# Routed experts: how the first row tiles are filled, and when the residual is scaled

## The chip, the cores and the metric

The kernel runs on one core of a Trainium2 chip. It is one program for a whole network: a convolution block, a retention block, and two layers that each have an attention stage and a stage of 32 routed experts. The time is device microseconds (us) of one execution; lower is better. Three runs of the kernel before gave 2948.9, 2949.08 and 2956.04 us.

## The reference

Only the stage of the experts and the sum behind it matter here. Each token picks one of 4 groups and then 2 of the 8 experts of that group; an expert is a gated feed-forward (1024 to 512 to 1024), and its output is added to its tokens with a gate.

```python
def hier_moe(h, w_rg, b_rg, w_re, b_re, w1, w3, w2):
    ...                                    # router: expert (n, 2), gates (n, 2)
    order = jnp.argsort(flat_e)
    counts = jnp.bincount(flat_e, length=N_EXPERTS)
    ...                                    # tokens sorted by expert, empty slots left at token 0
    def run(args):
        xb, e = args
        return (jax.nn.silu(xb @ w1[e]) * (xb @ w3[e])) @ w2[e]
    ys = lax.map(run, (xs, block_e)).reshape(-1, d_)
    return jnp.zeros_like(h).at[slot_tok].add(ys * slot_gate[:, None])

# in each of the two layers l:
x = layer_norm(ALPHA * x + g1 * o_x, ln1_g[l], ln1_b[l])
hx = (x * (1 + sc2) + sh2).reshape(b_ * s_, d_)
...                                        # layer 0 also routes 256 context tokens
y = hier_moe(tokens, w_rg[l], b_rg[l], w_re[l], b_re[l], w1[l], w3[l], w2[l])
x = layer_norm(ALPHA * x + g2 * y[:b_ * s_].reshape(b_, s_, d_), ln2_g[l], ln2_b[l])
```

The kernel keeps `x` normalised but without `ln1_g` and `ln1_b`, so the last line needs `x * (ALPHA * ln1_g) + ALPHA * ln1_b`. The kernel calls this work on `x` the residual steps.

## The kernel before, in words

**Routing.** `route` works out where each token goes and ends with index lists on VectorE: `list0` holds for each of the 32 experts 128 row numbers (its first 128 tokens; an empty slot holds a number beyond the table, and the gather skips it), `list1` the places to scatter results to. The rows themselves lie in device memory, in `hxd`, 4 KB each.

**Experts.** `experts` goes through the 32 experts in a fixed order; `p` counts them. `fetch(p)` starts a gather of up to 128 rows into one of three row tiles `xg` (an indirect DMA that GpSimd issues). `prepare(p + 1, h)` turns half of the next expert's row tile on TensorE and copies it into `xT`: the first half on ScalarE, the second on VectorE (`self.turned` is that second copy). `narrow` computes 64 tokens: 64 small matmuls with w1 and w3 into two banks, Silu on ScalarE, a product `s` on VectorE, two transposes of `s`, a copy `sT` on VectorE, 16 matmuls with w2, a copy `y` on ScalarE, and a scatter. Where an expert has more than 64 tokens, a branch (`tc.If(v > BS)`) does the next 64 and so on; every engine passes this branch, and after it each waits until the others have done what stood ahead of it. While the first expert of a layer runs, `lists()` makes two more lists (`sw`, `gw`) for experts with over 128 tokens, in steps between its matmuls.

**Weights.** An expert has three tiles of 2 MB (w1, w3, w2), loaded in halves by `expert_tile` from the queue of SyncE (SP), at most four halves under way. There is room for eight tiles; a tile's load waits until TensorE is done with the tile eight places earlier. Eight are asked for before the first expert, three more behind each expert's branch.

**Residual.** `residual` is a generator that gets one step behind each expert. For each half `h` of the columns: two loads of 512 gains and offsets spread over 128 partitions (`res`, 256 KB each in the tile), then a scaling of both by ALPHA on VectorE (L1967), then one row tile of `x` per expert. Only the work on a row tile was tied to `self.turned` (a dependency that keeps it behind that copy). The other steps are put where the scheduler has place: it sorts each engine's instructions by its own estimate of when they are ready, within the stretch between two branches and with what has no open dependency pulled ahead.

**Start of a stage.** The row tiles lie in memory that the stage before used. `xg` is set to zero first (three memsets on GpSimd, L1891), since a gather leaves skipped rows as they are.

Of the kernel before, what the change touches and what calls it, by code (L numbers as in the profile page):

```python
# [14 lines left out]
I32 = mybir.dt.int32  # L15
# [6 lines left out]
P = 128  # L22
# [12 lines left out]

DEPTH = 3
PAGES = 23
ORDER = [g * EPG + i for i in range(EPG) for g in range(NG)]
BS = 64
NC_ = 2  # L40
# [78 lines left out]
class Net:  # L119
    GAIN, NP = 0.7, 13  # L120

    def __init__(self, ctx, tc, aps):
        self.ctx, self.tc, self.nc, self.a = ctx, tc, tc.nc, aps
        nc = self.nc
        self.n = 0
        self.cp = ctx.enter_context(tc.tile_pool(name="cp", bufs=1))
        self.ps = ctx.enter_context(tc.tile_pool(name="ps", bufs=8, space=PSUM))
        self.dp = ctx.enter_context(tc.tile_pool(name="dp", bufs=1, space=DRAM))
        self.ring = ctx.enter_context(tc.tile_pool(name="ring", bufs=4))
        lay, w = const_layout()  # L130
        self.clay = lay
        self.small = ctx.enter_context(tc.tile_pool(name="small", bufs=1))
        self.x = self.cp.tile([P, NT, D], F32, name="x")
        for t in range(NT):
            nc.sync.dma_start(self.x[:, t], aps["x"][0, t * P:(t + 1) * P])
        self.ident = self.const("ident", self.cp)
        self.ctx_t = self.cp.tile([P, NC_, D], F32, name="ctx_t")
        self.gate = self.cp.tile([P, NT + NC_, 2], F32, name="gate")
        self.place = self.cp.tile([P, 2 * (NT + NC_)], F32, name="place")
        self.lists = self.cp.tile([P, NE], I32, name="list0"), self.cp.tile([P, 2 * NE], I32, name="list1")  # L140
        self.cnt = self.cp.tile([P, NE], I32, name="cnt")
        self.bg = deque()
        self.credit, self.gain = 0.0, 0.65
        self.pre = {}
# [1519 lines left out]
    def route(self, l, nt):  # L1664
# [61 lines left out]
        nc.vector.scalar_tensor_tensor(f, u, half, f, op0=ALU.mult, op1=ALU.add)  # L1726
        ts(u, f, tok + 0.5, float(tok), op0=ALU.is_ge, op1=ALU.mult)
        tt(u, f, u, op=ALU.subtract)
        ts(f, f, 0.5, 1e6, op0=ALU.is_lt, op1=ALU.mult)
        nc.vector.scalar_tensor_tensor(self.lists[0], u, -1.0, f, op0=ALU.add, op1=ALU.add)  # L1730
        ts(m, v, 0.5, 1e6, op0=ALU.is_lt, op1=ALU.mult)
# [49 lines left out]
    def experts(self, l, nt):  # L1781
# [32 lines left out]
        def gather(x, src, idx):  # L1814
            nc.gpsimd.indirect_dma_start(out=x, out_offset=None, in_=src,  # L1815
                                         in_offset=bass.IndirectOffsetOnAxis(ap=idx, axis=0),
                                         bounds_check=src.shape[0] - 1, oob_is_err=False)

        def scatter(y, dst, idx):
            nc.gpsimd.indirect_dma_start(out=dst, out_offset=bass.IndirectOffsetOnAxis(ap=idx, axis=0), in_=y,  # L1820
                                         in_offset=None, bounds_check=dst.shape[0] - 1, oob_is_err=False)
# [11 lines left out]
        def narrow(xT, i, w1, w3, w2, aside=iter(()), turn=lambda h: None):  # L1833


            hs = [self.bank(), self.bank()]
            tok = slice(i * BS, (i + 1) * BS)
            for h, w in zip(hs, (w1, w3)):
                for k in range(KD):
                    for c in range(2):  # L1840
                        mm(h[c * BS:(c + 1) * BS, 0:256], lhsT=xT[:, k, tok], rhs=w[:, k, c * 256:(c + 1) * 256],  # L1841
                           start=k == 0, stop=k == KD - 1, skip_group_check=True, tile_position=(0, c * BS))
                    next(aside, None)
            deque(aside, 0)
            s = new("s", 256, 1)
            nc.scalar.activation(s, hs[0][:, :256], AF.Silu)  # L1846
            nc.vector.tensor_tensor(s, s, hs[1][:, :256], op=ALU.mult)  # L1847
            turn(0)
            sT = new("sT", 256, 1)
            vcopy(sT, flip(s, 2))  # L1850
            turn(1)
            b = self.bank()
            for k in range(4):
                o = (k % 2) * P + (k // 2) * BS
                for c in range(2):
                    mm(b[c * BS:(c + 1) * BS], lhsT=sT[:, o:o + BS], rhs=w2[:, 2 * k + c], start=k == 0, stop=k == 3,  # L1856
                       skip_group_check=True, tile_position=(0, c * BS))
            y = new("y", 512, 2)
            acopy(y, b)  # L1859
            return y  # L1860
# [24 lines left out]
            scatter(broad(xT, part), yw, idx)  # L1885

        col = lambda t, e, i, n: t[:, e * n + i:e * n + i + 1]
        AHEAD = 2
        xg = [bc.tile([P, D], F32, name=f"xg{i}") for i in range(AHEAD + 1)]
        for x in xg:  # L1890
            nc.gpsimd.memset(x, 0.0)  # L1891
        xT, vs = {}, {}

        def fetch(p):

            if p < NE:
                e = ORDER[p]
                vs[e] = nc.values_load(cnt[0:1, e:e + 1], min_val=0, max_val=tok)
                gather(xg[p % (AHEAD + 1)], hw, col(gidx, e, 0, 1))

        def prepare(p, h):

            if p < NE:
                x = xg[p % (AHEAD + 1)]
                c = slice(h * 512, (h + 1) * 512)
                if h == 0:
                    xT[p] = new("xT", D, 2)
                    acopy(xT[p][:, c], flip(x[:, c], 4))
                else:
                    self.turned = vcopy(xT[p][:, c], flip(x[:, c], 4)).ins  # L1910
# [13 lines left out]
        for p, e in enumerate(ORDER):  # L1924
            with tc.high_priority():
                fetch(p + AHEAD)
            w = [self.wt.pop((e, m)) for m in range(3)]
            part = lambda m, i, w=w: w[m][:, i]
            v, x = vs.pop(e), xT.pop(p).rearrange("p (k s) -> p k s", k=KD)
            label = f"more_{l}_{p}"  # L1930
            hint = lambda i: tc.mark_branch_hint_location(f"{label}_{i}", 0, engines=[mybir.EngineType.PE])
            if p:
                hint("")
            scatter(narrow(x, 0, *w, lists() if p == 0 else iter(()), lambda h: prepare(p + 1, h)), yd, col(sidx, e, 0, 2))

            with tc.If(v > BS, preferred_fallthrough_block=True, label=label + "_"):  # L1936
                hint(0)
                more = new("wx", D, 1)
                with tc.If(v > 2 * BS, preferred_fallthrough_block=False):
                    gather(more, hw, col(gw, e, 1, nt))  # L1940
                scatter(narrow(x, 1, *w), yd, col(sidx, e, 1, 2))
                with tc.If(v > 2 * BS, preferred_fallthrough_block=True, label=label + "_0"):
                    hint(1)
                    rows128(more, col(sw, e, 1, nt), part)
                    with tc.If(v > 4 * BS, preferred_fallthrough_block=True, label=label + "_1"):
                        hint(2)
                        gather(more, hw, col(gw, e, 2, nt))
                        rows128(more, col(sw, e, 2, nt), part)
                        with tc.If(v > 6 * BS, preferred_fallthrough_block=True, label=label + "_2"):
                            with tc.For_i(3, (v + 2 * BS - 1) // (2 * BS), 1) as i:  # L1950
                                block(more, e, i, part)
            while self.wq_ and self.wn < 3 * (p + 1) + 8:
                self.expert_tile()
            next(residual, None)
            if p == NE - 3:
                self.combine_start(l, nt)

    def residual(self, l, nt):

        nc = self.nc  # L1960
        vs = [self.tmp.tile([P, 512], F32, tag=f"res{i}", name=self.nm("res"), bufs=1) for i in range(2)]
        for h in range(2):
            for v, k in zip(vs, ("ln1_g_2", "ln1_b_2")):
                nc.sync.dma_start(v, self.a[k][l, h * 512:(h + 1) * 512].partition_broadcast(P))
            yield
            for v in vs:
                nc.vector.tensor_scalar(v, v, ALPHA, None, op0=ALU.mult)  # L1967
            for t in range(nt):
                yield
                xs = self.rows(t)[:, h * 512:(h + 1) * 512]  # L1970
                op = nc.vector.tensor_tensor(xs, xs, vs[0], op=ALU.mult)
                dep = mybir.DependencyInfo(mybir.DependencyClass.Sync, mybir.DependencyReason.DATA)
                self.tc.add_manual_dep(op.ins, self.turned.name, dep, reason="one tile with each expert")
                nc.vector.tensor_tensor(xs, xs, vs[1], op=ALU.add)

    def combine_start(self, l, nt):
# [82 lines left out]
```

## Time and profile before

| | us |
|---|---|
| median of three runs | 2949.08 |
| the profiled execution | 2948.09 |
| its span on the core | 2945.8 |
| experts of layer 0, first row tile's transposes | 1355.39 |
| experts of layer 1, first row tile's transposes | 2272.94 |
| TensorE matmuls busy | 2557.8 |
| VectorE busy | 1318.4 |
| GpSimd busy | 618.2 |

Times in the rows below are microseconds from the start of the span. PE is TensorE, DVE VectorE, ACT ScalarE, POOL GpSimd, SP SyncE; SPq is the queue that issues transfers. The 2.3 us between the span and the execution's own time lie outside what the engines do. Layer 0's experts stand at 1355 to 1925 us, layer 1's at 2273 to 2899 us.

### The profile page before, as it was taken

To read this page: it belongs to the slowest core of one execution; us is meant where nothing else is said; L and a number is where in the kernel's file an instruction comes from. 1 tells how busy PE (TensorE), PEld (TensorE's weight loads), DVE (VectorE), ACT (ScalarE), POOL (GpSimd) and SP (SyncE) were. 2 spreads that over 40 slices of the span, in tenths; PEclk is the share of its full clock that TensorE was granted. 3 is DMA by queue.
4 is the path that set the end of the run, shared out by engine and by line. 5 is a ranking of instruction groups with operands and counts; after the bars stand their busy time and mean duration, and the time that the engine had idled before them with its cause. 6 is when DMAs were issued, how large, how long until landed. Compare 5 with 4: busy or idle time off the path is not lost. (4 is left out here: it accounts for less than half of the span.)

```text
span 2945.8 us, 38452 instructions
## 1 busy us (share of the span) xinstructions
PE 2557.8 (87%) x14392; PEld 1673.1 (57%) x14392; DVE 1318.4 (45%) x2803; ACT 790.8 (27%) x1750; POOL 618.2 (21%) x577
## 2 busy tenths in 40 slices
PE   5899989999999899995988888878796798888884
PEld 4666657787776785673544444447565454344442
DVE  6999975455355636763111111164876111010104
ACT  5666643223223324420101101023341011010100
POOL 4777740000001200142111111010414111010101
PEclk9999999999999999997999999989897999999997
DMA  6121244424422127324999999842224899475995
GB/s 193 58 86 62 82 172 150 144 90 147 162 100 72 36 47 257 79 108 185 393 399 394 391 404 397 323 159 65 65 57 165 326 390 403 170 312 234 394 405 214
DMA packets 202089, 610.39 MB, mean 207 GB/s; under 512 B 38542, under 2 KB 64538, under 8 KB 168932
## 3 DMA queue, kind: packets, MB, share of 16 engines
q1 hardware_dynamic: 179780, 572.10, 51.4%
q0 software_dynamic: 20400, 31.48, 3.3%
q8 instruction: 194, 3.18, 0.4%
q10 hardware_dynamic: 1520, 2.03, 0.2%
q14 instruction: 195, 1.60, 0.1%
HBM read 611.85 MB, written 29.20 MB: 218 GB/s over the span
## 5 line engine op out<-in xcount | busy, mean ns | idle before, releaser
L1841 PE MATMUL ps<-w,xT 128*64 128x256 f32 x4928 | 570.6, 384 | 82.4 <-ACTq L1936 41.0
L1841 PEld LDWEIGHTS ps<-w,xT 128*64 128x64 f32 x4928 | 348.6, 137 | 313.4 <-ACTq L1936 84.2
L1847 DVE TENSOR_TENSOR s<-s,ps 128x256 f32<-128x256 f32 x77 | 32.5, 422 | 860.3 <-PE ps L1841 860.3
L1856 PE MATMUL ps<-w,sT 128*64 128x512 f32 x1232 | 284.1, 603 | 23.9 <-DVE sT L1850 13.7
L425 POOL TENSOR_TENSOR c<-c,q 128x512 f32<-128x512 f32 x190 | 254.9, 1342 | 107.0 <-ACT q L424 94.7
L431 DVE SCALAR_TENSOR_TENSOR ps<-u,dwT,ps 128x512 f32<-128x512 f32 x274 | 201.0, 744 | 0.7
L282 PE MATMUL ps<-w,w 128*128 128x512 f32 (+1 forms) x480 | 182.1, 381 | 14.1 <-ACT w L243 12.8
L297 DVE TENSOR_TENSOR w<-w,w 128x256 fp32r<-128x256 f32 x288 | 186.1, 663 | 17.6 <-ACT w L296 17.3
L284 PE MATMUL ps<-w,w 128*128 128x512 f32 (+1 forms) x480 | 179.4, 376 | 10.2 <-DVE w L297 9.5
L1856 PEld LDWEIGHTS ps<-w,sT 128*64 128x64 f32 x1232 | 83.7, 137 | 174.8 <-issue 133.2
L1859 ACT COPY y<-ps 128x512 f32<-128x512 f32 x77 | 45.1, 586 | 506.4 <-PE ps L1856 506.4
L283 PE MATMUL ps<-w,w 128*128 128x512 f32 (+1 forms) x480 | 180.4, 376 | 0.0
L1820 POOL DMA_INDIRECT yd<-y,list x77 | 76.9, 999 | 457.5 <-ACTq L1936 236.1
L1815 POOL DMA_INDIRECT xg<-hxd,list x64 | 66.2, 1034 | 504.7 <-PE ps L1830 494.7
L284 PE MATMUL ps<-hT,w 128*128 128x512 f32 x384 | 151.1, 417 | 14.8 <-DVE w L297 14.6
L282 PE MATMUL ps<-hT,w 128*128 128x512 f32 x384 | 154.4, 404 | 9.2 <-ACT w L296 9.2
L283 PE MATMUL ps<-hT,w 128*128 128x512 f32 x384 | 151.6, 397 | 0.0
L424 ACT ACTIVATE q<-u,dwT 128x512 f32<-128x512 f32 x190 | 130.9, 719 | 1.2 <-POOL c L425 1.1
L1846 ACT ACTIVATE s<-ps 128x256 f32<-128x256 f32 x77 | 29.6, 384 | 309.4 <-PE ps L1841 306.5
L282 PEld LDWEIGHTS ps<-w,w 128*128 128x128 f32 x480 | 93.2, 195 | 32.8 <-ACT w L243 15.2
L916 POOL DMA_DIRECT2D small<-in_consts_dram x5 | 2.7, 548 | 507.8 <-ACT w L243 507.8
L284 PEld LDWEIGHTS ps<-w,w 128*128 128x128 f32 x480 | 93.2, 195 | 28.3 <-DVE w L297 11.3
(497 smaller groups left out, 4589.0 us busy)
## 6 DMA issues: line engine op xcount, KB each, us to landing
w<-in_w_dram SPq DMA_DIRECT2D x384, 1024.0 KB
w<-in_w_ada_dram SPq DMA_DIRECT2D x24, 2048.0 KB
w<-in_conv_w_in_dram SPq DMA_DIRECT2D x16, 1024.0 KB
w<-in_ret_w_in_dram SPq DMA_DIRECT2D x8, 2048.0 KB
w<-in_w_in_dram SPq DMA_DIRECT2D x6, 2048.0 KB
w<-yd SPq DMA_DIRECT2D x20, 512.0 KB
w<-in_conv_w_in_dram SPq DMA_DIRECT2D x4, 2048.0 KB
w<-in_conv_w_out_dram SPq DMA_DIRECT2D x4, 2048.0 KB
```

The source lines that it names most:

```text
L282: mm(out, lhsT=sh, rhs=mh, start=first, stop=False)
L283: mm(out, lhsT=sh, rhs=ml, start=False, stop=False)
L284: mm(out, lhsT=sl, rhs=mh, start=False, stop=last)
L297: nc.vector.tensor_tensor(view(l), raw, view(h).bitcast(F32), op=ALU.subtract)
L424: nc.scalar.activation(q, u[:, t:t + S], AF.Copy, scale=w(t))
L425: nc.gpsimd.tensor_tensor(cs[m], cs[m], q, op=ALU.add)
L431: nc.vector.scalar_tensor_tensor(acc, u[:, t:t + S], w(t), acc, op0=ALU.mult, op1=ALU.add)
L1815: nc.gpsimd.indirect_dma_start(out=x, out_offset=None, in_=src, in_offset=bass.IndirectOffsetOnAxis(ap=idx, axis=0), bounds_check=src.shap ...
L1820: nc.gpsimd.indirect_dma_start(out=dst, out_offset=bass.IndirectOffsetOnAxis(ap=idx, axis=0), in_=y, in_offset=None, bounds_check=dst.shap ...
L1841: mm(h[c * BS:(c + 1) * BS, 0:256], lhsT=xT[:, k, tok], rhs=w[:, k, c * 256:(c + 1) * 256], start=k == 0, stop=k == KD - 1, skip_group_che ...
L1856: mm(b[c * BS:(c + 1) * BS], lhsT=sT[:, o:o + BS], rhs=w2[:, 2 * k + c], start=k == 0, stop=k == 3, skip_group_check=True, tile_position=( ...
L1859: acopy(y, b)
```

## The change

It does four things.

1. The three memsets of `xg` are gone. For the first three experts of a layer the gather takes its rows from a list of its own, `early` (three columns, made by three more VectorE instructions in `route`), in which an empty slot holds row 0. So these three gathers move 128 rows each.
2. The residual generator gets its first step behind the third expert, not the first, and has one more empty step between the two loads and their scaling.
3. The two scalings are tied to `self.turned` too.
4. What is left of `lists()` is emptied behind `narrow`, not inside it. `lists()` has 12 steps in layer 0 and 8 in layer 1, `narrow` asks 16 times, so nothing is ever left.

```diff
+AHEAD = 2
...
+        self.early = self.cp.tile([P, AHEAD + 1], I32, name="early")
...  in route
         tt(u, f, u, op=ALU.subtract)
+
+        for p in range(AHEAD + 1):
+            ts(self.early[:, p:p + 1], u[:, ORDER[p]:ORDER[p] + 1], -1.0, 0.0, op0=ALU.add, op1=ALU.max)
         ts(f, f, 0.5, 1e6, op0=ALU.is_lt, op1=ALU.mult)
         nc.vector.scalar_tensor_tensor(self.lists[0], u, -1.0, f, op0=ALU.add, op1=ALU.add)
...  in narrow
-            deque(aside, 0)
...  in experts
-        AHEAD = 2
         xg = [bc.tile([P, D], F32, name=f"xg{i}") for i in range(AHEAD + 1)]
-        for x in xg:
-            nc.gpsimd.memset(x, 0.0)
...
-                gather(xg[p % (AHEAD + 1)], hw, col(gidx, e, 0, 1))
+                gather(xg[p % (AHEAD + 1)], hw, self.early[:, p:p + 1] if p <= AHEAD else col(gidx, e, 0, 1))
...
-            scatter(narrow(x, 0, *w, lists() if p == 0 else iter(()), lambda h: prepare(p + 1, h)), yd, col(sidx, e, 0, 2))
+            late = lists() if p == 0 else iter(())
+            scatter(narrow(x, 0, *w, late, lambda h: prepare(p + 1, h)), yd, col(sidx, e, 0, 2))
+            deque(late, 0)
...
-            next(residual, None)
+            if p > 1:
+                next(residual, None)
...  in residual
             yield
+            yield
+
+            def after(op):
+                dep = mybir.DependencyInfo(mybir.DependencyClass.Sync, mybir.DependencyReason.DATA)
+                self.tc.add_manual_dep(op.ins, self.turned.name, dep, reason="one step with each expert")
+
             for v in vs:
-                nc.vector.tensor_scalar(v, v, ALPHA, None, op0=ALU.mult)
+                after(nc.vector.tensor_scalar(v, v, ALPHA, None, op0=ALU.mult))
             for t in range(nt):
                 yield
                 xs = self.rows(t)[:, h * 512:(h + 1) * 512]
-                op = nc.vector.tensor_tensor(xs, xs, vs[0], op=ALU.mult)
-                dep = mybir.DependencyInfo(mybir.DependencyClass.Sync, mybir.DependencyReason.DATA)
-                self.tc.add_manual_dep(op.ins, self.turned.name, dep, reason="one tile with each expert")
+                after(nc.vector.tensor_tensor(xs, xs, vs[0], op=ALU.mult))
                 nc.vector.tensor_tensor(xs, xs, vs[1], op=ALU.add)
```

How it moves instructions shows at three places. The first is VectorE at the end of the first expert of layer 0, before the change; `s` and `sT` are the product and its copy that the matmuls with w2 wait for, `xT` is the second half of the next expert's turned rows, `res` the gains and offsets, and the load of `cnt` begins the branch.

```order
L1811 TENSOR_TENSOR lm<-ps_11055,lm 128x192
L1847 TENSOR_TENSOR s_11152<-s_11152,ps_11047 128x256
L1812 TENSOR_SCALAR gw<-lm 128x192
L1967 TENSOR_SCALAR res_11477<-res_11477 128x512
L1850 COPY sT_11162<-ps_11163 128x256
L1967 TENSOR_SCALAR res_11478<-res_11478 128x512
L1910 COPY xT_11155<-ps_11167 128x512
L1898 TENSOR_LOAD cnt
```

The same place after the change:

```order
L1816 TENSOR_TENSOR lm<-ps_11056,lm 128x192
L1851 TENSOR_TENSOR s_11153<-s_11153,ps_11048 128x256
L1817 TENSOR_SCALAR gw<-lm 128x192
L1854 COPY sT_11163<-ps_11164 128x256
L1911 COPY xT_11156<-ps_11168 128x512
L1899 TENSOR_LOAD cnt
```

Both scalings of `res` have left the first expert; one of them stood ahead of `sT`. They now stand behind `xT` of the fifth expert.

The second place is VectorE at the end of the first expert of layer 1, before the change, where the same names mean the same.

```order
L1910 COPY xT_26097<-ps_26109 128x512
L1967 TENSOR_SCALAR res_26419<-res_26419 128x512
L1967 TENSOR_SCALAR res_26420<-res_26420 128x512
L1898 TENSOR_LOAD cnt
L1936 COMPARE_AND_BRANCH
```

The same place after the change:

```order
L1851 TENSOR_TENSOR s_26095<-s_26095,ps_26010 128x256
L1854 COPY sT_26105<-ps_26106 128x256
L1911 COPY xT_26098<-ps_26110 128x512
L1899 TENSOR_LOAD cnt
L1939 COMPARE_AND_BRANCH
```

Here the scalings stood behind `xT` but ahead of the branch; they too are now at the fifth expert. On SP the first two loads of `res` keep their place, ahead of the first branch, in both layers.

The third place is GpSimd at the start of the experts of layer 0, before the change; the first `xg` is the first expert's tile, the second the second's, the third the third's.

```order
L1891 MEMSET xg_10976 128x1024
L1891 MEMSET xg_10977 128x1024
L1891 MEMSET xg_10978 128x1024
L1815 DMA xg_10976<-hxd_10105,list_79 128x1024
L1815 DMA xg_10978<-hxd_10105,list_79 128x1024
L1815 DMA xg_10977<-hxd_10105,list_79 128x1024
```

After the change (the tiles are now 10980, 10981 and 10982, in that order of experts):

```order
L1820 DMA xg_10982<-hxd_10106,early 128x1024
L1820 DMA xg_10980<-hxd_10106,early 128x1024
L1820 DMA xg_10981<-hxd_10106,early 128x1024
L1820 DMA xg_10980<-hxd_10106,list_79 128x1024
L1820 DMA xg_10981<-hxd_10106,list_79 128x1024
```

The memsets are gone, and the third expert's gather now goes ahead of the first expert's. In layer 1 the same rows stand in the same order.

## Rows read from the trace of the kernel before

**Rows 1.** Stretches of the expert stages (--windows): length, busy us per engine, clock, DMA.
```profile
core 0: us, PE busy (x) PEld busy (x) DVE busy (x) ACT busy (x) POOL busy (x), PEclk, DMA share, GB/s
1381.00:1387.00 6.00, 6.00 (x20) 1.83 (x22) 0.75 (x2) 0.08 (x1) 0.00 (x0) 0.61 0.00 0
1399.00:1925.00 526.00, 461.05 (x3356) 246.12 (x3356) 73.42 (x148) 55.39 (x108) 66.91 (x66) 1.00 0.97 380
2316.00:2330.00 14.00, 12.23 (x88) 6.01 (x84) 0.85 (x2) 1.53 (x3) 1.03 (x1) 1.00 0.11 41
```
**Rows 2.** DVE in time, layer 0's first expert (start, us, form, idle before).
```profile
1380.06 0.43 DVE L1967 TENSOR_SCALAR res<-res 128x512 f32<-128x512 f32 x1 [10.38 <-DMA res<-in_ln_g_dram]
1380.40 0.42 DVE L1850 COPY sT<-ps 128x256 f32<-128x256 f32 x1
```
**Rows 3.** PE in time, layer 0's first expert.
```profile
1369.57 0.44 PE L1830 MATMUL ps<-c_ident,s 128*128 128x128 f32 x2
1380.87 6.00 PE L1856 MATMUL ps<-w,sT 128*64 128x512 f32 x16 [10.43 <-DVE sT L1850]
1386.70 7.07 PE L1841 MATMUL ps<-w,xT 128*64 128x256 f32 x64
1394.38 0.44 PE L1830 MATMUL ps<-c_ident,s 128*128 128x128 f32 x2 [0.60 <-DVE s L1847]
1395.33 1.08 PE L1856 MATMUL ps<-w,sT 128*64 128x512 f32 x4 [0.52 <-DVE sT L1850]
```
**Rows 4.** SP's queue: what it waited for (us, times, longest), 1330 to 1420 us.
```profile
SPq L1646 <- PEq L1942: 24.2, 1, 24.2
```
**Rows 5.** SP's transfers in time, 1372 to 1400 us.
```profile
1372.98 0.33 SPq L1964 DMA_DIRECT2D res<-in_ln_g_dram  x1
1399.12 0.90 SPq L1646 DMA_DIRECT2D w<-in_w_dram  x2
```
**Rows 6.** DVE in time, layer 1's first expert.
```profile
2286.77 0.69 DVE L1910 COPY xT<-ps 128x512 f32<-128x512 f32 x1
2301.79 0.43 DVE L1967 TENSOR_SCALAR res<-res 128x512 f32<-128x512 f32 x1 [0.81 <-DMA res<-in_ln_b_dram]
```
**Rows 7.** PE in time, end of layer 1's first expert and start of its second.
```profile
2286.81 3.65 PE L1856 MATMUL ps<-w,sT 128*64 128x512 f32 x16
2302.69 9.35 PE L1841 MATMUL ps<-w,xT 128*64 128x256 f32 x64 [12.22 <-DMA w<-in_w_dram]
```
**Rows 8.** What PE waited for (us, times, longest), 1399 to 1925 us.
```profile
PE ps L1841 <- ACTq L1936: 20.1, 23, 1.0
```
**Rows 9.** POOL in time, start of layer 0's experts, then of layer 1's.
```profile
1347.15 2.78 POOL L1891 MEMSET xg<- 128x1024 f32 x3 [15.65 <-DVE list L1730]
1350.11 1.17 POOL L1815 DMA_INDIRECT xg<-hxd,list  x1 [0.18 <-POOL xg L1891]
...
2266.85 2.90 POOL L1891 MEMSET xg<- 128x1024 f32 x3 [12.79 <-DVE scol L1755]
2269.92 1.10 POOL L1815 DMA_INDIRECT xg<-hxd,list  x1 [0.17 <-POOL xg L1891]
```
**Rows 10.** DVE in time, end of layer 0's lists.
```profile
1346.68 0.19 DVE L1730 SCALAR_TENSOR_TENSOR list<-small 128x32 int32<-128x32 f32 x1
```
**Rows 11.** PE in time, first transposes of either layer's experts.
```profile
1355.39 1.94 PE L1830 MATMUL ps<-c_ident,xg 128*128 128x128 f32 x8 [10.22 <-DMA xg<-hxd,list]
...
2272.94 1.94 PE L1830 MATMUL ps<-c_ident,xg 128*128 128x128 f32 x8 [8.09 <-DMA xg<-hxd,list]
```
**Rows 12.** DMA queues (packets, MB, share of engines): 2271-2273, 1352-1354, 1351.5-1356.5, 1378-1380 us.
```profile
q0 software_dynamic: 208, 0.00, 5.1%
...
q0 software_dynamic: 206, 0.34, 60.8%
...
q0 software_dynamic: 429, 0.62, 44.4%
...
q1 hardware_dynamic: 157, 0.28, 38.2%
```
**Rows 13.** DVE in time, scaling of the second half in layer 0.
```profile
1544.53 0.43 DVE L1967 TENSOR_SCALAR res<-res 128x512 f32<-128x512 f32 x1 [0.34 <-DVEq L1942]
```

## The prediction, made before the changed kernel had run

> **What bounds the kernel now.** I read the stages first, by stretches [rows 1]. Through layer 0's experts the transfers are busy 97% of the time at 380 GB/s, and TensorE 461 of 526 us: 32 experts of 6 MB are streamed, and the end of the stage is when the stream began plus its length. So what counts is not busy time but anything that lets the stream begin later than it could. Such places are at the start of each layer's experts, and the timelines of the engines show two.
>
> In layer 0, VectorE is stuck for 10.38 us in front of the first scaling of `res`, whose load has not landed, and the copy `sT`, queued behind it, starts only at 1380.40 [rows 2]. [...] The wait reaches the stream: SP stands 24.2 us waiting for TensorE [rows 4], with all eight places for weights taken, and issues the next weights at 1399.12 [rows 5]. Loading waits for TensorE, and TensorE for a vector that nobody needs yet.
>
> In layer 1 the scalings stand behind `xT`, so nothing of the first expert is behind them, but the branch is. VectorE ends the second scaling at 2301.79 + 0.43 = 2302.22 [rows 6]; TensorE has been done since 2286.81 + 3.65 = 2290.46 and starts the second expert at 2302.69 [rows 7], 0.47 us after VectorE. The row names a weight transfer as releaser, which I don't believe (a rival below). Here the stream had data to fetch until 2316 and stood nearly idle until 2330, 11% busy [rows 1], again for want of places.
>
> **The change part by part.** All sums are against the profiled execution, 2948.09 us, of which 2945.8 are the span; the median of the runs is 1.0 us above it.
>
> *Scalings out of layer 0's first expert.* The two transposes of `s` start at 1369.57. In the next block of 64 tokens the matmuls with w2 follow the start of those transposes by 1395.33 - 1394.38 = 0.95 us [rows 3]. So they can start at 1370.52 instead of 1380.87: 10.35 us. They then take 3.65 us as in rows 7, not 6.00, since the engine doesn't idle: 2.35 more. Together 12.7 us. What is late next: the weights of the first two experts are there (the load of `res` went out at 1372.98 behind them all [rows 5]), and SP waits for TensorE, so stream and TensorE move by the same 12.7.
>
> *Scalings out of layer 1's first expert.* Where the next expert waits only for the branch, the gap is 20.1/23 = 0.87 us [rows 8]. So the second expert starts at 2290.46 + 0.87 = 2291.33 and not at 2302.69: 11.36 us. Its first 64 matmuls took 9.35 us after the idle time [rows 7] against 7.07 [rows 3]: 2.28. Together 13.6 us. The limit behind it is the stream, which has older loads until about 2316 and could gain 14 us there [rows 1]; 13.6 less what the start loses (next) fits.
>
> *Memsets, lists and gathers.* The memsets take 2.78 and 2.90 us on GpSimd, straight ahead of the first gather [rows 9]. Three instructions of 128x1 come in ahead of the last list, whose own 0.19 us [rows 10] is the nearest duration; side by side I take 0.4 us for the three, between 0 and 0.6. The gathers then start at 1347.55 and 2267.25. But two things get dearer: the third expert's tile goes first, and every tile has 128 rows. TensorE's first transposes thus wait for 2 x 128 x 4096 B = 1.05 MB. With hardly a row to fetch, start of gather to first transpose took 2272.94 - 2269.92 = 3.0 us in layer 1 [rows 9, 11] (208 packets moved 0.00 MB there [rows 12]). For the bytes the trace gives 0.34 MB in the 2 us in which layer 0's first gather ran at its fullest, 0.17 MB/us; as a lower end 0.62 in 5 us, 0.124, which has gaps in it [rows 12]; as an upper end the weights' 380 GB/s [rows 1]. I take 0.17, the nearest: the same queue, rows of the same size. That is 6.2 us, so transposes at 1347.55 + 3.0 + 6.2 = 1356.75 (1.4 later than 1355.39) and 2276.45 (3.5 later than 2272.94 [rows 11]). The ends are 8.5 us (3.7 and 5.8 later) and 2.8 us (2.0 earlier and 0.1 later). In layer 0 the 2.8 us of memset are about paid back in bytes; in layer 1, where the first expert had almost no rows, the change costs.
>
> [...]
>
> *Moved and tied steps.* The scalings (0.43 us each [rows 2]) now stand behind `xT` in the fifth expert. From there VectorE has nothing to do for the expert in hand while TensorE does 3.65 us of w2, so they are covered; without that cover they would cost 0.9 us a layer. Their loads keep their place on SP, so no load of weights moves; they land some 40 us before use. The second half's loads go three experts later; before, its scaling waited 0.34 us for the branch and not for data [rows 13], and the distance of load and use is kept. Emptying `lists()` later changes nothing.
>
> *Sum.* 12.7 - 1.4 + 13.6 - 3.5 = 21.4 us: 2926.7 against the profiled execution, 2927.7 against the median, say 2928. With the ends of the gather: 26.3 - 9.5 = 16.8 gives 2932; 26.3 + 1.9 = 28.2 gives 2921. Own range of this case 2921 to 2933.
>
> **The rivals.**
>
> *Fast tiles.* The three gathers run side by side at the weights' rate, since no weights move then. 2921, or a little below if the fixed part shrinks too. For it: engines were 60.8% busy at the fullest [rows 12]. Against: the fullest rate seen is under half of 380.
>
> *Layer 1 really waits for weights.* The row names them [rows 7]. Then only layer 0's part is left, and the dearer starts: 12.7 - 1.4 - 3.5 = 7.8, 2941. Against: TensorE started 0.47 us behind VectorE, and the second expert's weights were asked for before the first expert ran.
>
> *The stall moves.* VectorE reaches a scaling of the second half before its load has landed; tied behind `xT` and ahead of the branch, it holds up the next expert as in layer 1 now. The price is at most the flight of such a load, 1380.06 - 1372.98 = 7.1 us [rows 2, 5], in each layer: 2928 + 7 to 2928 + 14. Against: [rows 13].
>
> *Slower than before.* All empty slots read one row. If that row's memory serves the engines one by one, the first tile comes so late that it eats the rest. The point is where 256 rows take 16 to 17 us (3.0 + 17.5 us from 1347.55 makes up the 12.7, 16.3 us in layer 1 the 13.6), some 15 rows per us; at 20 us the kernel would be 6 us slower, 2955. Against: the load of `res` reads one 2 KB line 128 times and moved 157 packets in 2 us [rows 12], 78 per us.
>
> *It does not do what it says* is ruled out: the order shows the scalings gone from both first experts.
>
> **How the numbers follow.** Forecast 0.66; fast tiles 0.13; layer 1 waits for weights 0.08; stall moves 0.10; slower 0.03. The predicted time is 2928 us. The range is 2917 to 2938: it takes in the ends of the gather, a little below the fast tiles, and one moved stall; outside are most of the weights' rival, two moved stalls, and the slow row. A measurement of this kernel can tell about 0.3%, 8.8 us, from no change, so faster means under 2940.2: the forecast, fast tiles, most of the moved stalls and a part of the weights' rival, 0.90. Within 0.3%: the rest of both, 0.07. Slower: 0.03.
>
> **What would show it right or wrong.** In the changed profile VectorE has no wait for `res` over 1 us; in layer 0 the first matmuls with w2 follow the transposes of `s` by about 1 us and take 3.65; SP's wait for TensorE shrinks from 24.2 to some 12; in layer 1 TensorE starts the second expert 0.9 us behind the first, and the idle stretch of the stream around 2316 to 2330 is nearly gone. The first transposes come 9.2 us after the start of the first gather in both layers; if they come after 6 or 12, the bytes were mis-sized. I am wrong if TensorE still stands some 10 us in either place, with another releaser, or if stages that come later take back what was gained here.

## The result, and the profile after

The changed kernel took 2935.06 us (median of 5 runs, 2933.25 to 2936.51) against 2950.36 (median of 5 runs) for the kernel before: ratio 0.9946, 95% interval 0.9932 to 0.9959, so 12 to 20 us faster. Forecast were 2928 us, a gain of 21.4. The profiled execution took 2936.2 us, of which 2934.0 are the span, 11.8 less than before.

The stages first, as in [rows 1] (us in the stretch, busy time and instructions of PE, PEld, DVE, ACT and POOL, granted clock, share of the DMA engines, GB/s):

```profile
1375.00:1381.00 6.00, 6.00 (x58) 3.82 (x54) 0.00 (x0) 0.38 (x1) 1.03 (x1) 1.00 0.48 176
1393.00:1912.00 519.00, 455.70 (x3304) 241.42 (x3300) 73.66 (x147) 53.98 (x105) 65.71 (x65) 1.00 0.97 381
...
2299.00:2315.00 16.00, 14.28 (x98) 6.68 (x94) 1.12 (x3) 1.48 (x3) 1.87 (x2) 1.00 0.49 200
```

In layer 0 TensorE works without a pause at full clock where it stood at 0.61. In the poor stretch of layer 1's stream the transfers are busy 49% of the time, where it was 11%, so it is better and not gone. Layer 0 on VectorE and TensorE, against [rows 2, 3] (start, duration, what, idle time before it and what ended it):

```profile
1369.48 0.25 DVE L1817 TENSOR_SCALAR gw<-lm 128x192 int32<-128x192 f32 x1
1370.09 0.42 DVE L1854 COPY sT<-ps 128x256 f32<-128x256 f32 x1 [0.36 <-PE ps L1835]
1370.53 0.69 DVE L1911 COPY xT<-ps 128x512 f32<-128x512 f32 x1
```
```profile
1369.62 0.44 PE L1835 MATMUL ps<-c_ident,s 128*128 128x128 f32 x2
...
1370.57 3.65 PE L1860 MATMUL ps<-w,sT 128*64 128x512 f32 x16
1374.06 7.08 PE L1846 MATMUL ps<-w,xT 128*64 128x256 f32 x64
```

`sT` is copied at once, and the matmuls with w2 follow the transposes of `s` by 0.95 us and take 3.65; before, TensorE stood 10.43 us for `sT`, and they took 6.00 [rows 3]. SP's wait for TensorE, 24.2 us in [rows 4], is

```profile
SPq L1648 <- PEq L1945: 13.3, 1, 13.3
```

The gathers and the first transposes, against [rows 9, 11] (GpSimd's first gather of each layer and the two behind it in layer 0, then TensorE), and the queue that carried layer 0's tiles (packets, MB, share of 16 engines over 1346 to 1355 us), against [rows 12]:

```profile
1346.50 1.10 POOL L1820 DMA_INDIRECT xg<-hxd,early  x1 [16.59 <-DVE slow L1762]
1347.91 1.01 POOL L1820 DMA_INDIRECT xg<-hxd,early  x1 [0.30 <-issue]
1349.22 0.99 POOL L1820 DMA_INDIRECT xg<-hxd,early  x1 [0.30 <-issue]
...
2258.56 1.11 POOL L1820 DMA_INDIRECT xg<-hxd,early  x1 [13.72 <-DVE va L1809]
```
```profile
1354.51 1.73 PE L1835 MATMUL ps<-c_ident,xg 128*128 128x128 f32 x7 [10.91 <-DMA xg<-hxd,early]
...
2266.47 1.94 PE L1835 MATMUL ps<-c_ident,xg 128*128 128x128 f32 x8 [10.78 <-DMA xg<-hxd,early]
```
```profile
q0 software_dynamic: 432, 1.57, 51.6%
```

From the start of the first gather to the transposes it is 8.0 us in layer 0 and 7.9 in layer 1; of the 1.57 MB of all three tiles, 1.56 were on their way or in by then. Layer 1's first branch, against [rows 7], is where the forecast fails:

```profile
2280.66 3.65 PE L1860 MATMUL ps<-w,sT 128*64 128x512 f32 x16
2287.82 9.26 PE L1846 MATMUL ps<-w,xT 128*64 128x256 f32 x64 [3.51 <-PEq L1939]
```

TensorE waits for `res` no more, but it stands 3.51 us for its own sequencer (PEq), not 0.87, and the 64 matmuls behind it still take 9.26.

### The profile page after: what moved, and what is told of

It is laid out like the page before. It is cut to its first block, busy times and chain, and to the rows that moved or that the text cites. A ratio compares the mean times of both kernels' runs of the same rounds, so it can differ in the third digit from the quotient of the medians.

```text
span 2934.0 us, 38456 instructions
## 1 busy us (share of the span) xinstructions
PE 2559.1 (87%) x14392; PEld 1673.5 (57%) x14392; DVE 1313.5 (45%) x2809; ACT 790.7 (27%) x1750; POOL 610.5 (21%) x571
## 5 line engine op out<-in xcount | busy, mean ns | idle before, releaser
L284 PE MATMUL ps<-w,w 128*128 128x512 f32 (+1 forms) x480 | 184.0, 385 | 12.7 <-ACT w L245 11.5
L1820 POOL DMA_INDIRECT xg<-hxd,list x58 | 59.8, 1030 | 505.7 <-PE ps L1835 497.2
```

Of the source, the lines that this page charges most:

```text
L284: mm(out, lhsT=sh, rhs=mh, start=first, stop=False)
```

## The experiments

Times of a single kernel spread by up to 14 us, so beside the medians I read two local times from every trace: **L0** from the end of the last list (`list0` on VectorE) to the second group of w2 matmuls, the second block of layer 0's first expert; **L1** from the end of that list in layer 1 to the second expert's first w2 matmuls. **Stop** is TensorE's idle time behind layer 1's first expert, and **sixth** the time between the last w2 group of layer 1's sixth expert and the first of its seventh, where a second branch can stop TensorE. Two traces of one kernel differ by up to 1.3 us in L0 (`tie_only` and `tie_again`) and 0.9 in L1 (`after` and `after_again`). Each ratio is against runs of the kernel before that stood beside that kernel's own; their medians lie between 2950.36 and 2953.43.

| kernel | median us (runs) | ratio to before, 95% | L0 | L1 | stop | sixth |
|---|---|---|---|---|---|---|
| before | 2950.36 (5) | | 48.46 | 47.02 | 12.22 | 15.34 |
| after | 2935.06 (5) | 0.9946 (0.9932-0.9959) | 37.19 | 41.05 | 3.51 | 17.45 |
| after_again | 2934.81 (6) | 0.9933 (0.9917-0.9949) | 37.23 | 41.99 | 4.02 | 17.46 |
| res_only | 2935.01 (4) | 0.9943 (0.9920-0.9965) | 37.09 | 39.34 | 3.61 | 18.62 |
| gather_only | 2938.11 (6) | 0.9958 (0.9944-0.9972) | 37.50 | 45.67 | 7.60 | 14.09 |
| first_first | 2932.78 (4) | 0.9941 (0.9924-0.9957) | 34.27 | 40.28 | 3.55 | 17.16 |
| no_branch | 2925.08 (4) | 0.9907 (0.9891-0.9924) | 37.23 | 36.07 | 0 | 13.11 |
| hint_reg | 2935.70 (7) | 0.9951 (0.9937-0.9966) | 37.23 | 41.66 | 3.12 | 13.15 |
| best | 2933.39 (6) | 0.9947 (0.9932-0.9962) | 34.34 | 39.71 | 3.34 | 13.15 |
| memset_each | 2933.48 (6) | 0.9943 (0.9926-0.9961) | 35.04 | 40.59 | 2.92 | 17.22 |
| tie_only | 2930.65 (5) | 0.9947 (0.9928-0.9965) | 37.01 | 40.53 | 3.83 | 17.05 |
| tie_again | 2935.64 (6) | 0.9940 (0.9926-0.9955) | 35.75 | 40.36 | 3.54 | 17.25 |
| short_skip | 2919.02 (4) | 0.9880 (0.9863-0.9898) | 36.47 | 36.47 | 0.40 | 13.10 |
| loop_two | 2931.00 (6) | 0.9924 (0.9909-0.9940) | 37.20 | 41.08 | 3.34 | 13.16 |

**Half the change at a time.** `res_only` takes the gather half back:

```diff
-        for p in range(AHEAD + 1):
-            ts(self.early[:, p:p + 1], ...)
         xg = [bc.tile([P, D], F32, name=f"xg{i}") for i in range(AHEAD + 1)]
+        for x in xg:
+            nc.gpsimd.memset(x, 0.0)
...
-                gather(xg[p % (AHEAD + 1)], hw, self.early[:, p:p + 1] if p <= AHEAD else col(gidx, e, 0, 1))
+                gather(xg[p % (AHEAD + 1)], hw, col(gidx, e, 0, 1))
```

> The residual half of the change alone: memsets, row lists and the order of the first gathers as before. My prediction's sum for this half is 26.3 us, 2923. Theory A (read from the changed kernel's trace: layer 0 gains as forecast, layer 1's gain is cut by a stop of TensorE at the first expert's branch, 3.5 us and a colder clock behind it, 2 us): first transposes 8.5 and 6.4 us behind the end of the list as before, layer 1's second expert still starts 3 to 4 us behind the first expert's last matmuls, whole kernel 2930 to 2932, some 4 us under the full change. Rival B (the 128-row gathers ate what is missing): no stop in layer 1, 2923 to 2925.

2935.01, level with the whole change, so A's 2930 to 2932 was missed too, by 3 us. The stop is there (3.61), and a second one of 1.60 us within the 64 matmuls. Rival B is out; the gather half is worth nothing in layer 0 (37.09 against 37.19) and costs 1.7 us in L1. `gather_only` is the other half (the same lines the other way round, on the kernel before).

> The gather half alone: no memsets, 128-row tiles by the new list; the residual steps as before. My prediction priced this half at 4.9 us against: 2954. Theory A: it costs nothing by itself, because both first experts then wait for the load of res, which lands when it did; VectorE's wait for res gets shorter by what the tiles come later, within 1.5 us of before (2949 to 2952). Rival B: 128-row tiles delay both starts by themselves, 2955 or more.

A, the rival and the 4.9 us of my prediction were all wrong: this half is 12 us faster than before by itself, 2938.11. VectorE in layer 0 of this kernel:

```profile
1372.11 0.42 DVE L1855 COPY sT<-ps 128x256 f32<-128x256 f32 x1 [0.36 <-PE ps L1835]
1379.62 0.43 DVE L1969 TENSOR_SCALAR res<-res 128x512 f32<-128x512 f32 x1 [7.08 <-DMA res<-in_ln_g_dram]
```

The wait for `res` is still there, but `sT` is now ahead of it. Nobody wrote that order: with the memsets gone and three instructions added, the scheduler put the first scaling behind `sT` and no longer ahead of it. Which of the two edits moved it is not shown. So each half alone removes layer 0's wait (L0 37.09 and 37.50), and the two gains cannot be added.

**The tie alone.** The kernel before, plus:

```diff
             for v in vs:
-                nc.vector.tensor_scalar(v, v, ALPHA, None, op0=ALU.mult)
+                op = nc.vector.tensor_scalar(v, v, ALPHA, None, op0=ALU.mult)
+                dep = mybir.DependencyInfo(mybir.DependencyClass.Sync, mybir.DependencyReason.DATA)
+                self.tc.add_manual_dep(op.ins, self.turned.name, dep, reason="behind the turned tile")
```

> The kernel before with one thing more: the first two scalings are tied to the transposed copy of the next tile, in the same expert as before (no delay of two experts, memsets and lists as before). Theory A: what counts is that VectorE no longer meets the scalings ahead of sT and ahead of the first branch; both waits of TensorE for res go, as with the whole residual half, 2931 to 2937. Rival: the delay is needed too; VectorE meets the scalings in the second expert before res has landed and stands there 5 us or more with TensorE behind it, 2939 to 2945.

> The changed kernel once more, word for word, beside the next one on the same chip, and as a measure of how far two traces of one kernel differ in the stages that nobody touched: 2933 to 2937, both stops of TensorE in layer 1 in their places.

> The kernel that only ties the two scalings once more, in more rounds. If the gather half and the delay add nothing to the tie, it is level with the changed kernel or ahead by up to 5 us: 2929 to 2935. If its first median was luck, 2935 to 2938 and behind.

Theory A holds: over all runs the tie alone has a median of 2934.8 (11 runs) and the whole change 2935.1 (11 runs); the first median of `tie_only` was luck. VectorE met the scalings at 1395.8 in layer 0 and 2293.5 in layer 1, behind the next `xT` and without a wait. One dependency does what the whole change does; delay, list and missing memsets add nothing that can be measured.

**Order of the tiles.** In the changed kernel:

```diff
-        for p in range(AHEAD):
+        for p in range(AHEAD + 1):
             fetch(p)
...
-            with tc.high_priority():
-                fetch(p + AHEAD)
+            if p:
+                with tc.high_priority():
+                    fetch(p + AHEAD)
```

> The changed kernel, but the first expert's tile is gathered first and the third's last. Theory A: TensorE waits for 1.05 MB at 0.27 MB/us of which half is the third expert's; with its own tile first the transposes come 2.5 to 3.5 us earlier in both layers (5 to 6 us behind the start of the gather instead of 8.0), 5 to 6 us in all, 2929 to 2931. Rival: the three gathers share the queue's engines and end together whatever their order; transposes still 7.5 to 8 us behind the start, 2935.

GpSimd's first gather and TensorE's first transposes in layer 0:

```profile
1347.82 1.10 POOL L1820 DMA_INDIRECT xg<-hxd,early  x1 [16.58 <-DVE slow L1762]
```
```profile
1353.36 0.87 PE L1835 MATMUL ps<-c_ident,xg 128*128 128x128 f32 x3 [8.45 <-DMA xg<-hxd,early]
```

5.5 us behind the start (5.2 in layer 1), not 8.0: A's mechanism, though 2932.78 is 2 us above A's time. L0 gained 2.9 us, L1 only 0.8, since a second stop of 1.70 us showed up within the matmuls behind the branch. The median moved by 2.3, which is within the spread.

**The stop in layer 1.** `no_branch` puts `if p or not l:` ahead of the `tc.If(v > BS, ...)`.

> The changed kernel without the block for more than 64 tokens in layer 1's first expert, and without its branch (that expert has one token in these inputs, so the block does not run). Theory A: TensorE's stop of 3.5 us there is the fetch of code that the branch jumps to; without the jump the second expert starts under 1 us behind the first, its 64 matmuls take 7.1 us instead of 9.3, layer 1's third expert starts 5 to 6 us earlier, 2929 to 2931. Rival: the stop is a wait for data (weights, or the rows of the second expert) that the profile puts down to the branch; then 3 to 4 us of idle time stay in the same place with another releaser, 2934 to 2935.

`hint_reg` adds a hint at that place:

```diff
             if p:
                 hint("")
+            elif l:
+                tc.mark_branch_hint_location(f"{label}_", v, engines=[mybir.EngineType.PE])
```

> The changed kernel with a branch hint on TensorE for layer 1's first expert as the other experts have one, tied to the read of the count so that it stands just ahead of that expert. Theory A (the stop of 3.5 us is the fetch of the code behind the jump): the stop shrinks to about 1 us or less, the 64 matmuls behind it take 7.1 us and not 9.3, 2927 to 2932. Rival: a hint some 25 us ahead is lost again, or the stop is no fetch; TensorE stands 3.5 us as before, 2934 to 2936.

`short_skip` puts `if p or not l:` ahead of the two inner branches `tc.If(v > 2 * BS, ...)` alone.

> The changed kernel with the branch of layer 1's first expert kept, but most of what it jumps over left out (the nested blocks for more than 128 tokens, which do not run in these inputs; the second block of 64 stays). Theory A (the stop is the fetch of code that lies far behind the branch): with the target less than 200 TensorE instructions away the stop shrinks to about 1 us, as behind the other experts' branches, and the matmuls behind it take 7.1 us; some 5 us off layer 1, 2927 to 2932. Rival (every jump without a hint costs it, near or far): 3 us or more of idle time stay, 2933 to 2936.

The last w2 matmuls of the first expert and the start of the second, in `no_branch`, `hint_reg` and `short_skip`:

```profile
2283.35 3.65 PE L1860 MATMUL ps<-w,sT 128*64 128x512 f32 x16
2286.84 7.08 PE L1846 MATMUL ps<-w,xT 128*64 128x256 f32 x64
```
```profile
2280.18 3.65 PE L1860 MATMUL ps<-w,sT 128*64 128x512 f32 x16
2286.95 4.03 PE L1846 MATMUL ps<-w,xT 128*64 128x256 f32 x18 [3.12 <-PEq L1941]
```
```profile
2284.47 3.65 PE L1860 MATMUL ps<-w,sT 128*64 128x512 f32 x16
2288.53 7.13 PE L1846 MATMUL ps<-w,xT 128*64 128x256 f32 x64 [0.40 <-PEq L1939]
```

Without the jump there is no stop; with a jump over 164 TensorE instructions it is 0.40 us; with one over 380 it is 2.9 to 4.0. (The counts are of matmuls and weight loads in the kernel's code.) The data are the same in all, so the wait is not for data. The times confirm A but lie below its ranges: 2925.08 for 2929 to 2931 in `no_branch`, whose trace is of its slowest run, and 2919.02 for 2927 to 2932 in `short_skip`.

The record of the branch itself on TensorE's sequencer (PEldq; count, shortest, median and longest in ns, first and last start) says the same; here it is in the kernel before, the changed one and `short_skip`:

```profile
L1936 PEldq COMPARE_BRANCH  x1: 6157/6157/6157, 2287.3 to 2287.3; - x1
L1939 PEldq COMPARE_BRANCH  x1: 6166/6166/6166, 2281.1 to 2281.1; - x1
L1939 PEldq COMPARE_BRANCH  x1: 345/345/345, 2285.0 to 2285.0; - x1
```

The branch lasts 6.0 to 6.7 us in all twelve traces that jump over 310 or 380, that of the kernel before among them. It begins while TensorE still works on the first expert's w2 matmuls (in the changed kernel at 2281.1, with those matmuls until 2284.31), so only its end shows as a stop. In the changed kernel a queue of kind "instruction" brings one packet while TensorE stands (2284.5 to 2288 us); in `no_branch` it brings none from 2284 to 2290 us, and in `short_skip` the first one begins at 2288.6, when TensorE is at work again:

```profile
q8 instruction: 1, 0.02, 1.9%
```

In the ten traces that keep the jump and no longer wait for `res`, TensorE goes on 2.9 to 3.2 us after this packet begins. The second stop within the matmuls goes with the next packet of the same queue: in the seven traces that have such a stop that packet begins 2.6 to 3.5 us after TensorE has gone on, in the three that have none 1.1 to 1.5 us after. Why it comes later in some is open.

In the changed kernel the record of the same line is 0.07 us behind layer 1's second expert, which goes on without a jump, against 6.17 behind the first; in `short_skip` the first has 0.34. Where between 164 and 310 instructions the long record begins, no run shows.

The hint did not help. It ran at 2251.74, 28.5 us ahead of the branch, but the packet came behind the branch again, from 2284.05. Why is open. `hint_reg` moved all later code by a few instructions, and its trace has no stop behind the sixth expert (13.15 against 17.45). That the place of the code decides this is my reading and not shown: `memset_each` has the same hint and keeps that stop (17.22). `no_branch` and `short_skip`, which leave out code that these inputs don't run, gained more than L1 shows: both lost the stop behind the sixth expert, and in `short_skip` the 325-token expert took 72.5 us from its w2 matmuls to those of the next, where the others took 75.0 to 81.1.

**Two combinations.** `best` is `first_first` with the hint of `hint_reg`. `memset_each` is `res_only` with that hint, the order of `first_first` and

```diff
+                if p <= AHEAD:
+                    nc.gpsimd.memset(xg[p], 0.0)
                 gather(xg[p % (AHEAD + 1)], hw, col(gidx, e, 0, 1))
```

> That hint and the first expert's tile gathered first, together in the changed kernel. Theory A: both gains add up in layer 1, since the earlier transposes no longer run into the stop: first transposes 5.2 to 5.6 us behind the start of the gather, second expert under 1 us behind the first, 2922 to 2928. Rival: the weights' stream bounds layer 1 from there, and of the 5 us of the hint only 1 or 2 are left, 2929 to 2932.

> Residual half and hint as in the combined kernel, but the first tiles are cleared again, each just ahead of its own gather, with the old list (only rows that are used). By before's durations the first clearing is 0.95 us and hides the preparation of the gather; two stand ahead of the first gather, so it starts 2.0 to 2.3 us behind the end of the list, and lands after 5.3 us in layer 0 (before: 1350.11 to 1355.39) and 3.0 us in layer 1. Transposes 7.4 us behind the list's end in layer 0 and 5.2 in layer 1. Theory A: within 2 us of the combined kernel, 2922 to 2929. Rival (clearing costs its three instructions in full, as the change has it): 3 us or more behind it.

2933.39 and 2933.48, so the times of both missed: without a working hint there was nothing to add up. `memset_each` had its transposes 7.6 and 5.4 us behind the list, as `best` 6.6 and 5.9: clearing the first tiles costs as good as nothing once each tile is cleared ahead of its own gather.

**Less code, nothing left out.**

```diff
                     with tc.If(v > 4 * BS, preferred_fallthrough_block=True, label=label + "_1"):
-                        hint(2)
-                        gather(more, hw, col(gw, e, 2, nt))
-                        rows128(more, col(sw, e, 2, nt), part)
-                        with tc.If(v > 6 * BS, preferred_fallthrough_block=True, label=label + "_2"):
-                            with tc.For_i(3, (v + 2 * BS - 1) // (2 * BS), 1) as i:
-                                block(more, e, i, part)
+                        with tc.For_i(2, (v + 2 * BS - 1) // (2 * BS), 1) as i:
+                            block(more, e, i, part)
```

> The changed kernel with less code in every expert and nothing left out of the computation: tokens beyond 256 of an expert go through the loop that the kernel already has for those beyond 384, so one of the three copies of the 128-token block falls away in each of the 64 experts. The jump of layer 1's first expert then spans some 310 TensorE instructions instead of 380 (164 in the kernel with the short jump). Theory A (far targets cost a fetch): if 310 is near enough the stops of 3.5 us in layer 1 go, and with the one expert of 325 tokens 2 to 5 us slower in the loop the whole takes 2922 to 2930. Rival (310 is as far as 380): stops of 3 to 4 us stay, and the loop's cost shows alone, 2935 to 2940.

2931.0, between the two ranges, and the first stop stayed (3.34): 310 is as far as 380, so the rival was right there. The stop behind the sixth expert went (13.16), but one came up in layer 0, behind the second expert, where no other kernel here has one; the branch ahead of it lasts 6.63 us:

```profile
1405.24 8.81 PE L1846 MATMUL ps<-w,xT 128*64 128x256 f32 x64 [4.07 <-PEq L1939]
```

The 325-token expert took 81.1 us; the kernels without the loop took 72.5 to 80.2, so the loop's cost does not stand out of the spread. Of the kernels that compute everything for any routing it has the lowest ratio, with a median 4 us ahead of the change; the intervals overlap.

## Why the prediction was right or wrong

**What bounds the kernel, and layer 0: right.** The place of the scalings was the cause, and the stream moved with TensorE. L0 fell by 48.46 - 37.19 = 11.27 us; the forecast was 12.7 - 1.4 = 11.3. That the two agree so closely is luck: the gather cost 0.5 and not 1.4, and the first expert's matmuls, from the first transposes to those of `s`, took 15.11 us where they had taken 14.18 (granted clock 0.50 in the first 3.6 us and 0.94 in the rest, where it had been 0.58 and 1.00). `tie_only` and `tie_again`, one kernel, have 15.37 and 14.18 there.

**The gathers: right in sign, mis-sized.** I had the transposes 9.2 us behind the start of the gather; they came after 8.0 and 7.9. The start was later than I had it, 1.01 us behind the list's end and not 0.68. Behind the memsets the gather had followed within 0.18 us [rows 9], so some preparation on GpSimd may have been hidden under them; no run separates this. Measured from the list's end the transposes moved from 8.52 to 9.02 and from 6.38 to 8.89, 0.5 and 2.5 us later for 1.4 and 3.5. The bytes were mis-sized: 0.17 MB/us is too low, since 1.57 MB landed in the 6.2 us from the first packets, at 1348.3, to the transposes, 0.25 MB/us.

**Layer 1's branch: the step that failed.** "Where the next expert waits only for the branch, the gap is 20.1/23 = 0.87 us [rows 8]. So the second expert starts at 2290.46 + 0.87". It waited 3.51. I took the price of a branch from the other experts' rows; they have a hint and the first has none, and its record is 6.17 us where the median of the 64 on this line is 0.345. That it waits for the code behind the jump is theory A of `no_branch` and `short_skip`, whose stops of 0 and 0.40 us bear it out. The kernel before paid this too: its branch lasts from 2287.30 to 2293.46, under the 12.22 us of the row, where the wait for `res` covered it. So the price stood in the trace of before, and I did not look at the record of that branch. With the stop went the next term: "Its first 64 matmuls took 9.35 us after the idle time [rows 7] against 7.07 [rows 3]". They took 9.26, at a granted clock of 0.81 where it had been 1.00 ahead of the stop (the stretches before, in and behind the stop, columns as above):

```profile
2280.00:2284.00 4.00, 3.92 (x22) 1.40 (x20) 1.11 (x2) 0.32 (x1) 0.98 (x1) 1.00 1.02 422
2284.00:2288.00 4.00, 0.49 (x4) 0.21 (x4) 0.00 (x0) 0.58 (x1) 1.03 (x1) 0.99 1.00 403
2288.00:2297.00 9.00, 8.94 (x64) 5.54 (x61) 0.00 (x0) 0.38 (x1) 0.00 (x0) 0.81 1.02 397
```

(3.51 - 0.87) + (9.26 - 7.07) = 4.8 us lost, 1.0 given back by the gather, 0.3 lost by a slower first expert (13.24 us for 12.92 from its first transposes to those of `s`): L1 gained 47.02 - 41.05 = 6.0 and not 10.1. `no_branch`, with L1 at 36.07, shows that the rest was there to be had.

**The sum.** 11.27 + 5.97 = 17.2 of the 21.4 came, inside the measured 12 to 20. In the two profiled spans it is 11.8: another 1.4 came ahead of layer 0's list, and 2.1 were lost behind the sixth expert (below), 1.5 in the 325-token expert, 1.6 in layer 0's stream, 2.0 between layer 0's experts and layer 1's list; the rest is under 0.5. The last three are about the size by which traces of one kernel differ: `after` and `after_again` are 2.8, 1.1 and 2.5 us apart in them. The sixth expert is steady (17.45 and 17.46): its stop was 3.02 us before and 3.45 after, and the granted clock fell only behind the longer one, to 0.81 in the 64 matmuls against 1.00:

```profile
2397.31 7.13 PE L1841 MATMUL ps<-w,xT 128*64 128x256 f32 x64 [3.02 <-PEq L1942]
```
```profile
2382.75 8.81 PE L1846 MATMUL ps<-w,xT 128*64 128x256 f32 x64 [3.45 <-PEq L1945]
```

**The rivals.** The stall did not move: VectorE's idle time ahead of the scalings is 0.4 and 0.2 us in the changed kernel, and none of it for data. Layer 1 did not wait for weights: `no_branch` started its second expert without a pause behind the first. The tiles' rate, 0.25 MB/us, lies between the forecast's 0.17 and the 0.38 of the fast tiles, and did not show in the time. The range's lower end, 2917, allows for a shorter fixed part, and the changed kernel shows none: at 0.25 MB/us the 1.05 MB are 4.2 of the 8.0 and 7.9 us, which leaves 3.7 to 3.8 where the forecast had 3.0. Rereading one row was not slow: in layer 1, whose first expert has one token, the transposes came 7.9 us behind the start of the gather, in layer 0 8.0. What I had no rival for is what happened: another wait of TensorE behind the one that went.

**Moved and tied steps at nothing: right, and too modest.** The tie was the change. That the gather half would cost 4.9 us was wrong in the one way I had not looked for: I compared the order of before and after, but never asked which edit had moved which row.

## What to carry to other kernels

Where a scheduler sets the order, an edit can pay by moving another instruction; undo the edits one at a time before giving each its share, and look for the one dependency that pins the order. A long wait can hide a second one at the same place: ask what the engine would wait for if the first were gone, the branch there (6.16 us under 12.22 here) as well as the data. Take the price of a branch from its own record, or from branches that jump as far and are hinted alike.

## What the runs showed of the hardware

- The branch behind layer 1's first expert, taken over 380 or 310 TensorE instructions, lasted 6.0 to 6.7 us on TensorE's sequencer, over 164 instructions 0.34 us. TensorE stood 2.9 to 4.0 us for the far one in the ten traces that keep the jump and have no wait for `res` there (three of them with the hint that did not help), in seven with a second stop of 1.2 to 2.9 us within the next matmuls; over 164 instructions it stood 0.40 us. Behind the hinted branches in layer 0 of the kernel before it stood 0.87 us on average, by [rows 8] for ScalarE's sequencer.
- Where the 64 matmuls behind a stop of 3.27 to 4.07 us ran in one go (eleven cases) they took 8.44 to 9.79 us, in the changed kernel at a granted clock of 0.81 both times; behind the one of 3.02 us they took 7.13, at 1.00, as without a stop.
- A hinted branch stops TensorE in one kernel and not in another: the one behind the sixth expert of layer 1 did for 3.0 to 3.6 us in eight of the fourteen traces, the one behind layer 0's second expert for 4.07 us in `loop_two` alone. That the place of the code decides this is my reading and not shown.
- A gather of 128 rows of 4 KB reached TensorE 4.9 to 5.6 us after its issue when it was first of three (`first_first`, `best`), and 7.7 to 8.7 us after the issue of the first when it was second.
